# A gated two-layer MLP on one core: another order of the weight and x loads, matmuls on zeros at the start, transposes between the output blocks, and the last store in two halves

## The chip, the cores and the metric

The kernel runs on one core of one Trainium2 chip. The metric is device time in microseconds. All matmuls are done by TensorE (PE), which loads a 128x128 tile of one operand (PEld in the profile) and streams up to 512 columns of the other past it into PSUM. VectorE (DVE) and ScalarE (ACT) carry results from PSUM to SBUF, GpSimd (POOL) issues the loads, SyncE (SP) the stores.

## The reference

```python
# x: 16 x 256 x 512, w1: 512 x 4096, w2: 2048 x 512, all float32
h = x @ w1
gate, value = np.split(h, 2, axis=-1)
h = np.maximum(gate, 0) * value
return (h @ w2).astype(np.float32)
```

## The kernel before

The 16 x 256 tokens are taken as 4096 rows, in eight tiles of 512 (`TOK`). The program is written for the whole loop `for t in range(NT)`, without a hardware loop, and all matmuls are in fp16.

Both weights stay in SBUF. GpSimd's DMA converts float32 to fp16 on the way. It reads w1 in eight chunks of 512 columns (L74; chunks 0 to 3 are the gate half, 4 to 7 the value half), w2 in four chunks of 512 rows (L78), and x in tiles of 512 rows (L69). Each such load reads 1 MB and leaves 0.5 MB in SBUF. They stand in one queue, in the order of lines 87 to 104: x tile 0, w1 chunks 0 and 4, x tile 1, w1 1 and 5, x tile 2, w1 2 and 6, w2 0, x tile 3, w1 3 and 7, w2 1 to 3. GpSimd has eight semaphores for them, so that it issues the ninth load once the first has landed, and so on. x tiles 4 to 7 are asked for in the loop (L110), two tiles ahead; three buffers hold them.

A tile goes through three stages on PE:

- Transposes (L119): 16 of 128x128, four for each 128 columns of x. Four go into one PSUM tile `pt`, of which there are two, and DVE copies it into `xT` (L127).
- Stage 1 (L130 to L160): 16 blocks of 128 hidden columns. A block has four `pgate` matmuls, which ScalarE turns into `relu_sb` (L142), and four `pval` matmuls, which DVE multiplies with it into `g_sb` (L155). Blocks 0 to 3 need w1 chunks 0 and 4, blocks 4 to 7 chunks 1 and 5, and so on.
- Output stage (L162 to L177): four blocks `po` of 128 rows, each 16 matmuls of `g_sb` with w2 (L165), copied by ScalarE (L173) and stored by SP (L175). Matmuls 0 to 3 of a block need w2 chunk 0, matmuls 12 to 15 chunk 3.

Each engine runs its own instructions in the order in which a scheduler has put them, which is nearly that of the code; it lets a few matmuls of stage 1 slip in between the last transposes of a tile.

Of the kernel before, what the change touches and what calls it, by code (L numbers as in the profile page):

```python
# [11 lines left out]
BF16 = mybir.dt.bfloat16  # L12

MM_DT = FP16
STORE_ENGINE = "sync"


@with_exitstack
def kernel(
# [28 lines left out]

    const_pool = ctx.enter_context(tc.tile_pool(name="const", bufs=1))
    w_pool = ctx.enter_context(tc.tile_pool(name="weights", bufs=1))  # L50
    xf_pool = ctx.enter_context(tc.tile_pool(name="x_f16", bufs=3))
    xt_pool = ctx.enter_context(tc.tile_pool(name="xT", bufs=3))
    g_pool = ctx.enter_context(tc.tile_pool(name="g", bufs=2))
    r_pool = ctx.enter_context(tc.tile_pool(name="relu", bufs=6))
    o_pool = ctx.enter_context(tc.tile_pool(name="out_sb", bufs=6))
# [4 lines left out]

    identity = const_pool.tile([P, P], MM_DT, name="identity")
    make_identity(nc, identity)

    w1_sb = w_pool.tile([P, DB, H2], MM_DT, name="w1_sb")
    w2_sb = w_pool.tile([P, JB, C], MM_DT, name="w2_sb")

    def load_x_tile(t):
        x_f16 = xf_pool.tile([P, TB, D], MM_DT, name="x_f16")
        nc.gpsimd.dma_start(out=x_f16, in_=x_r[t])  # L69
        return x_f16  # L70

    def load_w1_chunk(ci, cols_per_chunk):
        cols = slice(ci * cols_per_chunk, (ci + 1) * cols_per_chunk)
        nc.gpsimd.dma_start(out=w1_sb[:, :, cols], in_=w1_r[:, :, cols])  # L74

    def load_w2_chunk(ci, jbs_per_chunk):
        jbs = slice(ci * jbs_per_chunk, (ci + 1) * jbs_per_chunk)
        nc.gpsimd.dma_start(out=w2_sb[:, jbs, :], in_=w2_r[:, jbs, :])  # L78

    W1_CHUNKS = 8  # L80
    w1_cols = H2 // W1_CHUNKS
    W2_CHUNKS = 4
    w2_jbs = JB // W2_CHUNKS

    x_tiles = {}

    x_tiles[0] = load_x_tile(0)
    load_w1_chunk(0, w1_cols)
    load_w1_chunk(4, w1_cols)
    if NT > 1:  # L90
        x_tiles[1] = load_x_tile(1)
    load_w1_chunk(1, w1_cols)
    load_w1_chunk(5, w1_cols)
    if NT > 2:
        x_tiles[2] = load_x_tile(2)
    load_w1_chunk(2, w1_cols)
    load_w1_chunk(6, w1_cols)
    load_w2_chunk(0, w2_jbs)
    if NT > 3:
        x_tiles[3] = load_x_tile(3)  # L100
    load_w1_chunk(3, w1_cols)
    load_w1_chunk(7, w1_cols)
    for ci in range(1, W2_CHUNKS):
        load_w2_chunk(ci, w2_jbs)

    for t in range(NT):
        if t not in x_tiles:
            x_tiles[t] = load_x_tile(t)
        for tp in (t + 1, t + 2):
            if tp < NT and tp not in x_tiles:  # L110
                x_tiles[tp] = load_x_tile(tp)

        x_f16 = x_tiles.pop(t)

        xT = xt_pool.tile([P, DB, TOK], MM_DT, name="xT")
        for db in range(DB):
            pt = pt_pool.tile([P, TB, P], MM_DT, name="pt")
            for tb in range(TB):
                nc.tensor.matmul(  # L119
                    pt[:, tb, :],  # L120
                    x_f16[:, tb, db * P:(db + 1) * P],
                    identity,
                    is_transpose=True,
                    start=(tb == 0),
                    stop=(tb == TB - 1),
                )
            nc.vector.tensor_copy(out=xT[:, db, :], in_=pt[:, :, :])  # L127

        g_sb = g_pool.tile([P, JB, TOK], MM_DT, name="g_sb")
        for jg in range(JB):  # L130
            pgate = ph_pool.tile([P, TOK], FP32, name="pgate")
            pval = ph_pool.tile([P, TOK], FP32, name="pval")
            for db in range(DB):
                nc.tensor.matmul(  # L134
                    pgate,
                    w1_sb[:, db, jg * P:(jg + 1) * P],
                    xT[:, db, :],
                    start=(db == 0),
                    stop=(db == DB - 1),
                )  # L140
            relu_sb = r_pool.tile([P, TOK], MM_DT, name="relu_sb")
            nc.scalar.activation(  # L142
                out=relu_sb,
                in_=pgate,
                func=mybir.ActivationFunctionType.Relu,
            )
            for db in range(DB):
                nc.tensor.matmul(  # L148
                    pval,
                    w1_sb[:, db, (JB + jg) * P:(JB + jg + 1) * P],  # L150
                    xT[:, db, :],
                    start=(db == 0),
                    stop=(db == DB - 1),
                )
            nc.vector.tensor_tensor(  # L155
                out=g_sb[:, jg, :],
                in0=relu_sb,
                in1=pval,
                op=mybir.AluOpType.mult,
            )  # L160

        for tb in range(TB):  # L162
            po = po_pool.tile([P, C], FP32, name="po")
            for jb in range(JB):
                nc.tensor.matmul(  # L165
# [4 lines left out]
                    stop=(jb == JB - 1),  # L170
                )
            out_sb = o_pool.tile([P, C], FP32, name="out_sb")
            nc.scalar.copy(out=out_sb, in_=po)  # L173
            if STORE_ENGINE == "sync":
                nc.sync.dma_start(out=out_r[t, :, tb, :], in_=out_sb)  # L175
            else:
                nc.gpsimd.dma_start(out=out_r[t, :, tb, :], in_=out_sb)  # L177


# [28 lines left out]
```

## Time and profile before

| | |
|---|---|
| device time, median of 4 runs | 365.66 us (364.35 to 366.6) |
| the profiled execution | 364.35 us |
| its span, first to last instruction | 362.4 us |
| PE matmul / weight load busy | 343.7 us (95%) / 158.1 us (44%) |
| DVE / ACT / POOL busy | 100.9 us / 96.4 us / 15.6 us |
| 128x512 matmuls, transposes | 1536, 128 |
| moved by DMA | 19.12 MB |

The profile shows one execution. A matmul's recorded time is longer than the time after which the next one starts, since they overlap in the array; so what a run of matmuls costs is read from the starts, and not from the mean of one. The timeline gives those starts, merged where instructions of one group follow each other. The chain that ended last gives, step by step from the end, what each piece of work waited for.

### The profile page before, as it was taken

What the parts mean: (1) busy time and instruction counts of PE and PEld (TensorE: products, weight loads), DVE (VectorE), ACT (ScalarE), POOL (GpSimd) and SP (SyncE); (2) the same over time, 40 slices, a digit from 0 to 9 for tenths busy, and PEclk for the clock granted to TensorE, in tenths of its full rate; (3) what the DMA queues carried; (4) which work ended last, traced back from release to release, by engine and by line L of the source; (5) the groups of instructions that cost most, each with busy time, mean ns of one, the idle gap of its engine ahead of it and who ended that gap; (6) DMA issues with size and microseconds to landing.
All of it is one profiled execution on the core that took longest, in us unless ns stands there. A gap on an engine that the chain in (4) does not pass through costs nothing.

```text
span 362.4 us, 4054 instructions
## 1 busy us (share of the span) xinstructions
PE 343.7 (95%) x1664; PEld 158.1 (44%) x1664; DVE 100.9 (28%) x160; ACT 96.4 (27%) x161; POOL 15.6 (4%) x26
## 2 busy tenths in 40 slices
PE   2996799999999999999999999999999999999996
PEld 1332344444444444444444444444444444444442
DVE  1333202333034420433113440243304332034400
ACT  1222212332123321333113331233212331133311
POOL 8320000000000000000000000000000000000000
PEclk9999999999999999999999999999999999999999
DMA  7999912300150002400023001100020000100002
GB/s 122 204 195 207 195 57 72 51 1 3 58 115 2 0 0 89 87 0 2 29 87 60 0 2 58 58 4 0 0 82 36 0 2 29 58 31 0 0 31 87
DMA packets 15185, 19.12 MB, mean 53 GB/s; under 512 B 832, under 2 KB 11072, under 8 KB 15168
## 3 DMA queue, kind: packets, MB, share of 16 engines
q0 software_dynamic: 10560, 10.49, 17.8%
q1 hardware_dynamic: 4608, 8.39, 6.1%
q8 instruction: 13, 0.21, 0.2%
q14 instruction: 4, 0.03, 0.0%
HBM read 20.97 MB, written 8.39 MB: 81 GB/s over the span
## 4 chain that ended last, share of the span: by engine, by line
PE 87%; DMA 9%; POOL 1%; DVE 1%; issue 0%; ACT 0%; POOLq 0%
PE po L165 30%; PE pval L148 28%; PE pgate L134 27%; DMA w_sb<-in_w_dram 9%; PE pt L119 2%; DVE xT L127 1%; POOL x_f L69 0%; POOL w_sb L74 0%; ACT out_sb L173 0%; POOL identity masks.py:199 0%; POOL identity masks.py:197 0%; POOLq masks.py:199 0%; POOLq L192 0%
## 5 line engine op out<-in xcount | busy, mean ns | idle before, releaser
L134 PE MATMUL pgate<-xT,w_sb 128*128 128x512 f16 x512 | 135.5, 384 | 2.2 <-DMA w_sb<-in_w_dram 2.2
L148 PE MATMUL pval<-xT,w_sb 128*128 128x512 f16 x512 | 132.5, 380 | 3.7 <-DMA w_sb<-in_w_dram 3.7
L155 DVE TENSOR_TENSOR g_sb<-relu_sb,pval 128x512 f16<-128x512 f16 x128 | 88.0, 687 | 142.9 <-PE pval L148 142.9
L142 ACT ACTIVATE relu_sb<-pgate 128x512 f16<-128x512 f32 x128 | 76.4, 597 | 163.8 <-PE pgate L134 163.8
L165 PE MATMUL po<-w_sb,g_sb 128*128 128x512 f16 x512 | 111.8, 380 | 0.0
L148 PEld LDWEIGHTS <-w_sb 128*128 128x128 f16 x512 | 49.8, 98 | 65.5 <-DMA w_sb<-in_w_dram 5.2
L134 PEld LDWEIGHTS <-w_sb 128*128 128x128 f16 x512 | 49.8, 98 | 61.5 <-DMA w_sb<-in_w_dram 3.3
L165 PEld LDWEIGHTS <-g_sb 128*128 128x128 f16 x512 | 50.0, 98 | 60.5
L173 ACT COPY out_sb<-po 128x512 f32<-128x512 f32 x32 | 18.7, 585 | 98.6 <-PE po L165 98.6
L127 DVE COPY xT<-pt 128x512 f16<-128x512 f16 x32 | 12.9, 422 | 102.1 <-PE pt L119 101.0
L119 PE MATMUL pt<-identity,x_f 128*128 128x128 f16 x128 | 11.7, 230 | 9.3 <-DMA x_f<-in_x_dram 7.1
L119 PEld LDWEIGHTS <-x_f 128*128 128x128 f16 x128 | 9.3, 103 | 12.8 <-DMA x_f<-in_x_dram 7.1
L69 POOL DMA_DIRECT2D x_f<-in_x_dram x8 | 6.1, 766 | 162.6 <-PE pt L119 160.3
L74 POOL DMA_DIRECT2D w_sb<-in_w_dram x8 | 6.0, 767 | 3.4 <-DMA w_sb<-in_w_dram 1.9
L78 POOL DMA_DIRECT2D w_sb<-in_w_dram x4 | 3.0, 741 | 7.9 <-DMA w_sb<-in_w_dram 5.2
L142 ACT ACT_TABLE_LOAD x1 | 1.3, 1283 | 0.7 <-PEq L192 0.7
masks.py:199 POOL TENSOR_SCALAR_AFFINE_SELECT identity<-identity 128x128 f16<-128x128 f16 x1 | 0.3, 305 | 0.1
masks.py:197 POOL MEMSET identity<- 128x128 f16 x1 | 0.2, 204 | 0.3 <-POOLq L192 0.3
L192 POOL MEMSET const-float32-0.0<- 128x1 f32 x1 | 0.1, 98 | 0.2 <-issue 0.2
L192 POOL MEMSET const-bfloat16-1.0<- 128x1 bf16 x1 | 0.1, 101 | 0.0
L192 POOL MEMSET const-uint8-127<- 128x1 uint8 x1 | 0.1, 101 | 0.0
L192 POOL MEMSET const-float32-1.0<- 128x1 f32 x1 | 0.1, 98 | 0.0
## 6 DMA issues: line engine op xcount, KB each, us to landing
out_dram<-out_sb SPq DMA_DIRECT2D x32, 256.0 KB, 2.0
w_sb<-in_w_dram POOLq DMA_DIRECT2D x12, 512.0 KB, 20.5
x_f<-in_x_dram POOLq DMA_DIRECT2D x8, 512.0 KB, 5.8
```

The costliest lines, as they stand in the source:

```text
L69: nc.gpsimd.dma_start(out=x_f16, in_=x_r[t])
L74: nc.gpsimd.dma_start(out=w1_sb[:, :, cols], in_=w1_r[:, :, cols])
L78: nc.gpsimd.dma_start(out=w2_sb[:, jbs, :], in_=w2_r[:, jbs, :])
L119: nc.tensor.matmul(pt[:, tb, :], x_f16[:, tb, db * P:(db + 1) * P], identity, is_transpose=True, start=(tb == 0), stop=(tb == TB - 1),)
L127: nc.vector.tensor_copy(out=xT[:, db, :], in_=pt[:, :, :])
L134: nc.tensor.matmul(pgate, w1_sb[:, db, jg * P:(jg + 1) * P], xT[:, db, :], start=(db == 0), stop=(db == DB - 1),)
L142: nc.scalar.activation(out=relu_sb, in_=pgate, func=mybir.ActivationFunctionType.Relu,)
L148: nc.tensor.matmul(pval, w1_sb[:, db, (JB + jg) * P:(JB + jg + 1) * P], xT[:, db, :], start=(db == 0), stop=(db == DB - 1),)
L155: nc.vector.tensor_tensor(out=g_sb[:, jg, :], in0=relu_sb, in1=pval, op=mybir.AluOpType.mult,)
L165: nc.tensor.matmul(po, g_sb[:, jb, tb * P:(tb + 1) * P], w2_sb[:, jb, :], start=(jb == 0), stop=(jb == JB - 1),)
L173: nc.scalar.copy(out=out_sb, in_=po)
L192: nc = _bacc.Bacc("TRN2", target_bir_lowering=False, num_devices=1)
```

## The change

- The order of the loads. Now it is x tile 0, all w1 chunks in the order 0, 4, 1, 5, 2, 6, 3, 7, w2 chunk 0, x tile 1, w2 chunks 1 to 3, x tile 2. x tiles 3 to 7 are asked for in the loop.
- DVE clears a tile `zeros` of 128x512, and PE multiplies it with itself 18 times ahead of the first transposes and 4 times behind them in the code, into a `pgate` buffer that nobody reads (`keep_warm`).
- The transposes of tile t+1 move from the start of tile t+1 into the output stage of tile t: four ahead of each `po` block (`transpose_group`). `xT` has two buffers instead of three.
- The last `po` block of the program is copied and stored in two halves of 256 columns. The copies of the output are left to the scheduler's choice of engine; it gives all of them to ScalarE, as before.
- `load_w1_chunk_staged` and its pool are defined, but nothing calls the function.

```diff
@@ -12,7 +12,6 @@
 BF16 = mybir.dt.bfloat16
 
 MM_DT = FP16
-STORE_ENGINE = "sync"
 
 
 @with_exitstack
@@ -48,8 +47,9 @@
 
     const_pool = ctx.enter_context(tc.tile_pool(name="const", bufs=1))
     w_pool = ctx.enter_context(tc.tile_pool(name="weights", bufs=1))
+    wst_pool = ctx.enter_context(tc.tile_pool(name="w_stage", bufs=2))
     xf_pool = ctx.enter_context(tc.tile_pool(name="x_f16", bufs=3))
-    xt_pool = ctx.enter_context(tc.tile_pool(name="xT", bufs=3))
+    xt_pool = ctx.enter_context(tc.tile_pool(name="xT", bufs=2))
     g_pool = ctx.enter_context(tc.tile_pool(name="g", bufs=2))
     r_pool = ctx.enter_context(tc.tile_pool(name="relu", bufs=6))
     o_pool = ctx.enter_context(tc.tile_pool(name="out_sb", bufs=6))
@@ -60,6 +60,14 @@
 
     identity = const_pool.tile([P, P], MM_DT, name="identity")
     make_identity(nc, identity)
+    zeros = const_pool.tile([P, 512], MM_DT, name="zeros")
+    nc.vector.memset(zeros, 0.0)
+
+    def keep_warm(n):
+        dummy = ph_pool.tile([P, TOK], FP32, name="pgate")
+        for _ in range(n):
+            nc.tensor.matmul(dummy, zeros[:, :P], zeros, start=True, stop=True)
+
 
     w1_sb = w_pool.tile([P, DB, H2], MM_DT, name="w1_sb")
     w2_sb = w_pool.tile([P, JB, C], MM_DT, name="w2_sb")
@@ -69,62 +77,61 @@
         nc.gpsimd.dma_start(out=x_f16, in_=x_r[t])
         return x_f16
 
-    def load_w1_chunk(ci, cols_per_chunk):
-        cols = slice(ci * cols_per_chunk, (ci + 1) * cols_per_chunk)
+    w1_cols = 512
+    W1_CHUNKS = H2 // w1_cols
+
+    def load_w1_chunk_swdge(ci):
+        cols = slice(ci * w1_cols, (ci + 1) * w1_cols)
         nc.gpsimd.dma_start(out=w1_sb[:, :, cols], in_=w1_r[:, :, cols])
 
-    def load_w2_chunk(ci, jbs_per_chunk):
-        jbs = slice(ci * jbs_per_chunk, (ci + 1) * jbs_per_chunk)
+    def load_w1_chunk_staged(ci):
+        cols = slice(ci * w1_cols, (ci + 1) * w1_cols)
+        w_stage = wst_pool.tile([P, DB, w1_cols], FP32, name="w_stage")
+        nc.sync.dma_start(out=w_stage, in_=w1_r[:, :, cols])
+        nc.any.tensor_copy(out=w1_sb[:, :, cols], in_=w_stage)
+
+    w2_jbs = 4
+    W2_CHUNKS = JB // w2_jbs
+
+    def load_w2_chunk_swdge(ci):
+        jbs = slice(ci * w2_jbs, (ci + 1) * w2_jbs)
         nc.gpsimd.dma_start(out=w2_sb[:, jbs, :], in_=w2_r[:, jbs, :])
 
-    W1_CHUNKS = 8
-    w1_cols = H2 // W1_CHUNKS
-    W2_CHUNKS = 4
-    w2_jbs = JB // W2_CHUNKS
-
+    def transpose_group(x_f16, xT, db):
+        pt = pt_pool.tile([P, TB, P], MM_DT, name="pt")
+        for tb in range(TB):
+            nc.tensor.matmul(
+                pt[:, tb, :],
+                x_f16[:, tb, db * P:(db + 1) * P],
+                identity,
+                is_transpose=True,
+                start=(tb == 0),
+                stop=(tb == TB - 1),
+            )
+        nc.vector.tensor_copy(out=xT[:, db, :], in_=pt[:, :, :])
+
+    keep_warm(18)
     x_tiles = {}
-
     x_tiles[0] = load_x_tile(0)
-    load_w1_chunk(0, w1_cols)
-    load_w1_chunk(4, w1_cols)
-    if NT > 1:
-        x_tiles[1] = load_x_tile(1)
-    load_w1_chunk(1, w1_cols)
-    load_w1_chunk(5, w1_cols)
+    for ci in (0, 4, 1, 5, 2, 6, 3, 7):
+        load_w1_chunk_swdge(ci)
+    load_w2_chunk_swdge(0)
+    x_tiles[1] = load_x_tile(1)
+    for ci in range(1, W2_CHUNKS):
+        load_w2_chunk_swdge(ci)
     if NT > 2:
         x_tiles[2] = load_x_tile(2)
-    load_w1_chunk(2, w1_cols)
-    load_w1_chunk(6, w1_cols)
-    load_w2_chunk(0, w2_jbs)
-    if NT > 3:
-        x_tiles[3] = load_x_tile(3)
-    load_w1_chunk(3, w1_cols)
-    load_w1_chunk(7, w1_cols)
-    for ci in range(1, W2_CHUNKS):
-        load_w2_chunk(ci, w2_jbs)
+
+    xT_cur = xt_pool.tile([P, DB, TOK], MM_DT, name="xT")
+    for db in range(DB):
+        transpose_group(x_tiles[0], xT_cur, db)
+    keep_warm(4)
+    x_tiles.pop(0)
 
     for t in range(NT):
-        if t not in x_tiles:
-            x_tiles[t] = load_x_tile(t)
         for tp in (t + 1, t + 2):
             if tp < NT and tp not in x_tiles:
                 x_tiles[tp] = load_x_tile(tp)
-
-        x_f16 = x_tiles.pop(t)
-
-        xT = xt_pool.tile([P, DB, TOK], MM_DT, name="xT")
-        for db in range(DB):
-            pt = pt_pool.tile([P, TB, P], MM_DT, name="pt")
-            for tb in range(TB):
-                nc.tensor.matmul(
-                    pt[:, tb, :],
-                    x_f16[:, tb, db * P:(db + 1) * P],
-                    identity,
-                    is_transpose=True,
-                    start=(tb == 0),
-                    stop=(tb == TB - 1),
-                )
-            nc.vector.tensor_copy(out=xT[:, db, :], in_=pt[:, :, :])
 
         g_sb = g_pool.tile([P, JB, TOK], MM_DT, name="g_sb")
         for jg in range(JB):
@@ -134,7 +141,7 @@
                 nc.tensor.matmul(
                     pgate,
                     w1_sb[:, db, jg * P:(jg + 1) * P],
-                    xT[:, db, :],
+                    xT_cur[:, db, :],
                     start=(db == 0),
                     stop=(db == DB - 1),
                 )
@@ -148,7 +155,7 @@
                 nc.tensor.matmul(
                     pval,
                     w1_sb[:, db, (JB + jg) * P:(JB + jg + 1) * P],
-                    xT[:, db, :],
+                    xT_cur[:, db, :],
                     start=(db == 0),
                     stop=(db == DB - 1),
                 )
@@ -159,7 +166,17 @@
                 op=mybir.AluOpType.mult,
             )
 
+        if t + 1 < NT:
+            xT_next = xt_pool.tile([P, DB, TOK], MM_DT, name="xT")
+            x_next = x_tiles[t + 1]
+        else:
+            xT_next = None
+
+        last_tile = t == NT - 1
         for tb in range(TB):
+            if xT_next is not None:
+                transpose_group(x_next, xT_next, tb)
+
             po = po_pool.tile([P, C], FP32, name="po")
             for jb in range(JB):
                 nc.tensor.matmul(
@@ -170,11 +187,19 @@
                     stop=(jb == JB - 1),
                 )
             out_sb = o_pool.tile([P, C], FP32, name="out_sb")
-            nc.scalar.copy(out=out_sb, in_=po)
-            if STORE_ENGINE == "sync":
+            if last_tile and tb == TB - 1:
+                half = C // 2
+                nc.any.tensor_copy(out=out_sb[:, :half], in_=po[:, :half])
+                nc.sync.dma_start(out=out_r[t, :, tb, :half], in_=out_sb[:, :half])
+                nc.any.tensor_copy(out=out_sb[:, half:], in_=po[:, half:])
+                nc.sync.dma_start(out=out_r[t, :, tb, half:], in_=out_sb[:, half:])
+            else:
+                nc.any.tensor_copy(out=out_sb, in_=po)
                 nc.sync.dma_start(out=out_r[t, :, tb, :], in_=out_sb)
-            else:
-                nc.gpsimd.dma_start(out=out_r[t, :, tb, :], in_=out_sb)
+
+        if xT_next is not None:
+            xT_cur = xT_next
+            x_tiles.pop(t + 1)
 
 
 # ---- launch: one core; inputs and outputs as the reference has them ----
```

GpSimd at the start of the program, before (`x_f` is an x tile; L74 is a chunk of w1, L78 one of w2):

```order
L69 DMA x_f_92<-in_x_dram 128x4x512
...
L74 DMA w_sb<-in_w_dram 128x4x512 x2
L69 DMA x_f_96<-in_x_dram 128x4x512
L74 DMA w_sb<-in_w_dram 128x4x512 x2
L69 DMA x_f_100<-in_x_dram 128x4x512
L74 DMA w_sb<-in_w_dram 128x4x512 x2
L78 DMA w_sb<-in_w_dram 128x4x512
L69 DMA x_f_105<-in_x_dram 128x4x512
L74 DMA w_sb<-in_w_dram 128x4x512 x2
L78 DMA w_sb<-in_w_dram 128x4x512 x3
```

And now (L77 is an x tile, L85 a chunk of w1, L98 one of w2):

```order
L77 DMA x_f_116<-in_x_dram 128x4x512
...
L85 DMA w_sb<-in_w_dram 128x4x512 x8
L98 DMA w_sb<-in_w_dram 128x4x512
L77 DMA x_f_127<-in_x_dram 128x4x512
L98 DMA w_sb<-in_w_dram 128x4x512 x3
L77 DMA x_f_132<-in_x_dram 128x4x512
L77 DMA x_f_478<-in_x_dram 128x4x512
```

The last two chunks of w1 were loads 12 and 13 of the queue and are 8 and 9; the last chunk of w2 was load 16 and is 14.

PE at the start of the program, with what it waits for (DMASW is a load, by the number of its semaphore; Pool and DVE are those engines); before, the transposes of x tile 0 and the first gate matmuls:

```order
L119 LDWEIGHTS x_f_92 [waits DMASW0_49]
L119 MATMUL pt<-identity,x_f_92 128x128 [waits Pool_49]
...
L119 MATMUL pt<-identity,x_f_92 128x128 [waits DVE_49]
...
L134 LDWEIGHTS w_sb [waits DMASW1_49]
L134 MATMUL pgate<-xT,w_sb 128x512
```

And now, where the matmuls on `zeros` stand first (22 of them, two rows each):

```order
L69 LDWEIGHTS zeros [waits DVE_49]
L69 MATMUL pgate<-zeros 128x512
...
L103 LDWEIGHTS x_f_116 [waits DMASW0_49]
L103 MATMUL pt<-identity,x_f_116 128x128 [waits Pool_49]
...
L141 LDWEIGHTS w_sb [waits DMASW1_49]
L141 MATMUL pgate<-xT,w_sb 128x512
```

All 22 matmuls on `zeros` come ahead of the first transpose, the four that are written behind the transposes too.

PE from the end of stage 1 of tile 0 to the first gate matmuls of tile 1, before, the first row of each piece (DMASW7 is the last chunk of w2; `x_f_96` is x tile 1):

```order
L148 MATMUL pval<-xT,w_sb 128x512
...
L165 MATMUL po<-w_sb,g_sb 128x512 [waits DMASW1_49]
...
L165 MATMUL po<-w_sb,g_sb 128x512 [waits DMASW7_49]
...
L165 MATMUL po<-w_sb,g_sb 128x512 [waits Activation_49]
...
L119 MATMUL pt<-identity,x_f_96 128x128 [waits PE_49]
...
L119 MATMUL pt<-identity,x_f_96 128x128 [waits DVE_49]
...
L134 MATMUL pgate<-xT,w_sb 128x512
...
L119 MATMUL pt<-identity,x_f_96 128x128 [waits DVE_49]
```

And now (DMASW5 is the last chunk of w2, DMASW2 is x tile 1, `x_f_127`):

```order
L155 MATMUL pval<-xT,w_sb 128x512
L103 LDWEIGHTS x_f_127 [waits DMASW2_49]
L103 MATMUL pt<-identity,x_f_127 128x128 [waits PE_49]
...
L182 MATMUL po<-w_sb,g_sb 128x512 [waits DMASW1_49]
...
L182 MATMUL po<-w_sb,g_sb 128x512 [waits DMASW5_49]
...
L103 MATMUL pt<-identity,x_f_127 128x128 [waits PE_49]
...
L182 MATMUL po<-w_sb,g_sb 128x512
...
L103 MATMUL pt<-identity,x_f_127 128x128 [waits DVE_49]
...
L182 MATMUL po<-w_sb,g_sb 128x512 [waits Activation_49]
...
L141 MATMUL pgate<-xT,w_sb 128x512
```

The transposes of the next tile, which came in a row behind the fourth `po` block with waits on DVE among them, now come in groups of four ahead of each block.

## Rows read from the trace of the kernel before

**Rows 1.** The page: span, PE's share, DMA's busy tenths in 40 slices of the span.

```profile
span 362.4 us, 4054 instructions
...
PE 343.7 (95%) x1664; PEld 158.1 (44%) x1664; DVE 100.9 (28%) x160; ACT 96.4 (27%) x161; POOL 15.6 (4%) x26
...
DMA  7999912300150002400023001100020000100002
```

**Rows 2.** The page: the chain that ended last, share of the span by engine.

```profile
PE 87%; DMA 9%; POOL 1%; DVE 1%; issue 0%; ACT 0%; POOLq 0%
```

**Rows 3.** The chain in order of time, whole span: start us, us, what.

```profile
4.68 12.60 DMA w_sb<-in_w_dram
17.57 21.56 DMA w_sb<-in_w_dram
...
45.40 13.81 PE po L165 x64
...
345.08 13.83 PE po L165 x64
```

**Rows 4.** Waits, whole span: us in total, times, longest.

```profile
PE pval L148 <- DMA w_sb<-in_w_dram: 3.7, 3, 1.5
...
PE pgate L134 <- DMA w_sb<-in_w_dram: 2.2, 2, 1.8
```

**Rows 5.** Timeline of the start: start us, us, engine, line, what [idle before <-releaser].

```profile
0.74 0.20 POOL masks.py:197 MEMSET identity<- 128x128 f16 x1 [0.29 <-POOLq L192]
...
2.47 1.50 POOL L74 DMA_DIRECT2D w_sb<-in_w_dram  x2
...
7.14 2.14 PE L119 MATMUL pt<-identity,x_f 128*128 128x128 f16 x16 [7.14 <-DMA x_f<-in_x_dram]
...
9.65 3.59 PE L134 MATMUL pgate<-xT,w_sb 128*128 128x512 f16 x8 [0.37 <-DMA w_sb<-in_w_dram]
...
13.04 1.95 PE L148 MATMUL pval<-xT,w_sb 128*128 128x512 f16 x8
...
20.21 0.74 POOL L78 DMA_DIRECT2D w_sb<-in_w_dram  x1 [1.90 <-DMA w_sb<-in_w_dram]
...
23.72 0.74 POOL L78 DMA_DIRECT2D w_sb<-in_w_dram  x1 [2.77 <-DMA x_f<-in_x_dram]
...
45.23 2.11 PE L165 MATMUL po<-w_sb,g_sb 128*128 128x512 f16 x9
```

**Rows 6.** DMA issues begun near 3.2 and at 20.21: KB each, us to landing.

```profile
w_sb<-in_w_dram POOLq DMA_DIRECT2D x1, 512.0 KB, 8.9
...
w_sb<-in_w_dram POOLq DMA_DIRECT2D x1, 512.0 KB, 21.5
```

**Rows 7.** The chain from 59 to 63 us, between tiles 0 and 1.

```profile
59.21 0.24 PE pt L119 x4
...
59.47 0.43 DVE xT L127
...
59.95 0.38 PE pt L119 x4
60.33 0.22 PE pgate L134
60.55 0.22 PE pt L119 x4
...
62.31 0.86 PE pgate L134 x4
```

**Rows 8.** The page, costliest groups: count | busy us, mean ns of one | idle.

```profile
L173 ACT COPY out_sb<-po 128x512 f32<-128x512 f32 x32 | 18.7, 585 | 98.6 <-PE po L165 98.6
...
L119 PE MATMUL pt<-identity,x_f 128*128 128x128 f16 x128 | 11.7, 230 | 9.3 <-DMA x_f<-in_x_dram 7.1
```

**Rows 9.** The page, DMA issues: the stores, KB each, us to landing.

```profile
out_dram<-out_sb SPq DMA_DIRECT2D x32, 256.0 KB, 2.0
```

## The prediction

> **What bounds the kernel now.** I read the page's shares first, then the chain that ended last, then the waits of TensorE (PE), and last the timeline at the three places that the change touches. TensorE is busy for 95% of the span, and the DMA engines are busy only at its start [rows 1]. The chain is 87% PE and 9% DMA [rows 2]. So two things can give time: the PE's idle time while the weights come in, and PE work between the tiles that is not a needed 128x512 matmul.
>
> From tile to tile the output matmuls (`po`) start at 45.40 in tile 0 and at 345.08 in tile 7 [rows 3]: seven periods of 42.81 us. A `po` stage takes 13.81 us for 64 matmuls, 0.2158 each; four gate matmuls take 0.86 [rows 3, 7], the same pace. A tile has 128 + 64 = 192 such matmuls, 41.44 us. **1.37 us a tile** is the boundary: sixteen transposes and their waits.
>
> At the start PE waits for weights: 3.7 us in three waits ahead of `pval`, 2.2 us in two ahead of `pgate` [rows 4]. The first eight 128x512 matmuls, from 9.65 to 13.04, run at 0.424 us each, which is 512 columns at 1.2 GHz; from 13.04 on they run at the 2.4 GHz pace [rows 5]. PE's first work was at 7.14, so the clock rose 5.9 us after it. From 13.04 the rest of stage 1 needs 8 x 0.2158 + 28 x 0.863 = 25.90 us and would end at 38.94; the first `po` starts at 45.23 [rows 5]. So stage 1 of tile 0 loses **6.29 us** to late weights (the recorded waits plus a pipeline refill after each).
>
> **Load order.** Before, the 13th of 16 equal transfers (the last w1 chunk, landing at 17.57 + 21.56 = 39.13 [rows 3]) opens the last quarter of stage 1; three of the twelve ahead of it are x tiles 1 to 3, and one is a w2 chunk. Now that chunk is the 9th. The stream is one queue of 1 MB reads, so I give a transfer the landing time of its slot. Slot 3 lands at 3.2 + 8.9 = 12.1 (its issue is the second of the two that begin at 2.47), slot 5 at 4.68 + 12.60 = 17.28, slot 14 at 20.21 + 21.5 = 41.71 [rows 3, 5, 6]: 2.69 us a slot on average.
>
> Now PE's path through tile 0. The 22 zero matmuls (the 4 that are written after the transposes stand ahead of them too in PE's program) start when VectorE (DVE) has cleared `zeros`. The trace has no such clear on DVE; the nearest rows are the GpSimd clear of `identity`, 0.20 us from 0.74 [rows 5], and a DVE copy of 128x512, 0.43 us [rows 7], so they start between 0.94 and 1.2; I take 1.1. All at the slow pace they end at 1.1 + 22 x 0.424 = 10.4, all at the fast one at 5.9. With the rise 5.9 us after the first of them, 14 are slow and 8 fast, and they end near 8.8; I take that, since the 5.9 us is this kernel's own. x tile 0 has been there since 7.14 [rows 5], so its transposes begin 1.6 us later than before, but at the fast pace: as at a boundary, 1.34 us against the 2.14 us of the start [rows 5, 7]. The gate matmuls of the first two hidden blocks run from 10.1 to 11.9 and the value matmuls then wait for slot 3, to 12.2. So **the zero matmuls buy little**: the next weight chunk hides nearly all of it (12.2 instead of 13.04).
>
> From 12.2 stage 1 needs 25.90 us if no weight is late. Slot 5 (17.28) is wanted by the value matmuls of the fifth block at 18.2; later chunks have more room, since four blocks take 6.9 us and two slots 5.4. So it ends at 38.1. The output stage begins with four transposes (0.22), and its thirteenth matmul, at 38.1 + 0.22 + 12 x 0.2158 = 40.9, wants the last w2 chunk, slot 14, at 41.7: a **new wait of 0.8 us**, and the stage is pinned to the stream there. It ends, with 52 matmuls and three more groups of transposes, at 41.71 + 11.22 + 0.66 = 53.59. Without transposes and boundary that stands for a `po` start at 53.59 - 13.81 - 0.88 = 38.90 instead of 45.23: **6.3 us gained**. Before, the tail of w2 stayed hidden behind the late w1; that cover is gone, and the 0.8 us is its price. x tile 1 is slot 11, three before slot 14 and so near 33.6, ahead of its transposes at 38.1. Later x tiles are asked for more than one tile (over 40 us) ahead, as before.
>
> **Transposes.** Before, 16 of them run in a row between two tiles, and with two PSUM banks the third group waits for DVE's copy of the first (59.45 to 59.95) and the fourth is partly filled by a gate matmul [rows 7]. Now each group of four stands before one `po` block, 3.45 us after the group before; a copy of 0.43 us is done long before its bank is wanted, and the next tile's `xT` is complete 3 us early. What a group costs there is the four matmuls themselves: 0.22 us between two gate matmuls, 0.24 after `po` [rows 7]. No row shows a group followed by `po`; the bounds are zero (all four hidden) and 0.92, four times the recorded 230 ns of a transpose [rows 8]. I take 0.22, since the row at 60.55 also has weights loaded and 512-column matmuls on both sides. So 4 x 0.22 = 0.88 instead of 1.37 at seven boundaries: **3.4 us gained**. The copies fall into DVE's idle time beside `po`.
>
> **The last store** is now two halves. ScalarE copies 128x512 in 585 ns [rows 8]; a 128x256 copy is not in the trace, and lies between half of that and all of it. Two take 0.585 to 1.17 us; I take 0.74, as a copy has some cost that does not halve. SP is free, and its 256 KB stores land 2.0 us after issue [rows 9]. So the bounds are 1.0 gained (if half the bytes land in half the time) and 0.6 lost; with the landing left at 2.0 it is **0.15 us lost**.
>
> On this the Trainium skill, "DMA: Bandwidth & Descriptors", section "Anatomy of one DMA", says that most of a small transfer's 2 us is the receipt from the target memory and not the bytes, so that a half store would land no sooner. By that rule the split can't gain anything; the 2.0 us of the trace agrees in size, and no run here has a half store.
>
> **Sum.** 6.3 + 3.4 - 0.15 = 9.6 us. The profiled execution took 364.35 us, 1.95 more than its span of 362.4, so it would take 354.8. It was the fastest of the four runs shown; their median is 1.3 us higher, and I forecast the median: 365.66 - 9.6 = **356.0 us**.
>
> **Rivals.**
>
> *The zero matmuls don't raise the clock.* Then all 22 are slow and end at 10.4; transposes (2.14) and eight gates (3.4) stay slow, the value matmuls start at 16.0, stage 1 ends at 41.9, and nothing waits for w2. Tile 0 ends at 41.9 + 13.81 + 0.88 = 56.6, 3.0 us later: 359.0. For it: no row shows a matmul on zeros. Against: before, 16 transposes and 8 matmuls raised the clock. Chance 0.10.
>
> *The stream is slower than its slots.* GpSimd, which issues the ninth and later transfers as earlier ones land, was let go at 17.57, 20.21 and 23.72 [rows 3, 5]: one step took 2.6 us, the next 3.5. At 3.1 us a slot after slot 3, slot 14 lands at 46.2, 4.5 us later: 360.5. At 2.6 it lands at 40.7, nothing waits, and it is 355.2. Chance of a loss over 2 us: 0.12.
>
> *Slower: the transposes no longer overlap their neighbours.* If every transpose between `po` blocks is paid at its recorded 230 ns, a group costs 0.92 and not 0.22 and the 28 groups lose 19.6 us: 375.6. It decides from 0.56 us a group (9.6 / 28 more), and is slower by over 0.5% from 0.63. For it: the transposes now cut the densest stretch of the kernel 28 times. Against: the 0.22 and 0.24 us of rows 7. Chance 0.03.
>
> The Trainium skill, "TensorE: Matmul & The Clock Gate", Part 4, puts a transpose at about 275 ns in a kernel's context; an estimate by that figure is 1.1 us a group, 24.6 us lost over the 28. The trace speaks against taking it as occupancy: four starts pass in 0.22 us.
>
> *It doesn't do what it says.* The new order stands in the programs of PE and GpSimd, so that only a balance of losses (a late stream and dear transposes) could leave the time where it is: within 0.5%, chance 0.03.
>
> **How the numbers follow.** The forecast has 0.72, with 353.8 to 358.0 as its own range: 0.8 for the wait on w2, 1.0 gained or 0.6 lost at the last store, some 0.5 for the transposes, and the 1.3 us by which runs differ, which will not all fall on one side. The rest goes to 359.0, 360.5, no change and slower as above. A range of 353.8 to 360.0 takes in the cold start and most of the late stream. About 0.5% is what a measurement of this kernel can tell from no change: faster than 363.8 has 0.94, the same 0.03, slower 0.03.
>
> **What would show it.** Right: PE starts near 1.1 and the fast pace holds from the first gate matmul; only slot 3 and the last w2 chunk (about 0.8 us) are waited for by PE in tile 0; tile 0's `po` ends near 53.6; a period of 42.3 us with no wait of PE on DVE; the last copies some 0.15 us longer. Wrong: waits on w1 in stage 1 (the stream), eight gate matmuls at 0.42 us after 10 us (the clock), or a period over 42.8 us (the transposes).

## The result and the profile after

| | before | after |
|---|---|---|
| median | 365.25 us (16 runs, 363.65 to 366.98) | 354.93 us (10 runs, 354.66 to 355.8) |
| ratio after / before, 95% interval | | 0.9723 [0.9699, 0.9746] |
| span of the profiled execution | 362.4 us | 353.3 us |
| PE matmul busy | 343.7 us (95%) | 346.8 us (98%) |
| first `po` matmul of tile 0 (its start; the chain has 0.17 more) | 45.23 | 39.30 |
| last `po` matmul done, by the chain | 358.91 | 349.40 |
| from there to the end of the span | 3.49 us | 3.90 us |

The changed kernel is 10.3 us faster by the medians, and 9.1 us by the two spans. 356.0 us (353.8 to 360.0) was forecast; it came to 354.93.

The page after, its span, PE's row, the DMA slices and the chain by engine, beside [rows 1, 2]:

```profile
span 353.3 us, 4109 instructions
...
PE 346.8 (98%) x1686; PEld 160.0 (45%) x1686; DVE 101.0 (29%) x161; ACT 96.6 (27%) x162; POOL 15.6 (4%) x26
...
DMA  7999934000420006000150001100020000100011
...
PE 95%; DMA 3%; POOL 1%; ACT 0%; issue 0%; POOLq 0%
```

DMA's part of the chain has shrunk from 9% to 3%: it is what PE waits for at the start, once. The chain of tile 0 in order of time (start us, us, what), beside [rows 3, 7]:

```profile
3.22 9.90 DMA w_sb<-in_w_dram
...
13.17 1.90 PE pval L155 x8
...
39.24 0.22 PE pt L103 x4
39.47 3.45 PE po L182 x16
42.92 0.22 PE pt L103 x4
...
53.95 0.86 PE pgate L141 x4
...
81.80 3.45 PE po L182 x16
```

One load (`w_sb`, issued at 3.22) and then PE without a gap. From the `po` at 39.47 to the one at 81.80, tile 0 to tile 1, is 42.33 us; it was 42.81. Each group of four transposes takes 0.22 us between two `po` blocks, and there are no waits among them.

The start of the timeline (PE's matmuls, and three of the weight loads on zeros), beside [rows 5]:

```profile
1.19 7.47 PE L69 MATMUL pgate<-zeros 128*128 128x512 f16 x22 [1.19 <-DVE zeros L64]
...
1.60 0.15 PEld L69 LDWEIGHTS <-zeros 128*128 128x128 f16 x1 [0.28 <-issue]
2.02 0.15 PEld L69 LDWEIGHTS <-zeros 128*128 128x128 f16 x1 [0.28 <-issue]
...
6.29 1.88 PEld L69 LDWEIGHTS <-zeros 128*128 128x128 f16 x9 [0.28 <-issue]
...
8.50 0.61 PE L103 MATMUL pt<-identity,x_f 128*128 128x128 f16 x8
...
10.19 1.90 PE L141 MATMUL pgate<-xT,w_sb 128*128 128x512 f16 x8
...
13.17 1.90 PE L155 MATMUL pval<-xT,w_sb 128*128 128x512 f16 x8 [1.08 <-DMA w_sb<-in_w_dram]
```

PE now starts at 1.19. The weight loads on zeros come every 0.43 us (1.60, 2.02, ...) until 6.29, and then nine in 1.88 us: that is 1.2 GHz and then 2.4 GHz, some 5.1 us after the first matmul. The transposes and the first gate matmuls (8 in 1.90) run at the fast pace. Then PE waits 1.08 us for the third load, until 13.17. The waits of PE for loads over the whole span, beside [rows 4]:

```profile
PE pval L155 <- DMA w_sb<-in_w_dram: 1.1, 1, 1.1
```

Five waits were 5.9 us together; one of 1.1 us is left. The wait on the last w2 chunk, which was forecast, isn't there.

### The profile page after: what moved, and what is told of

Same layout as the page of the kernel before. It is cut to its first block, busy times and chain, and to the rows that moved or that the text cites. A ratio compares the mean times of both kernels' runs of the same rounds, so it can differ in the third digit from the quotient of the medians.

```text
span 353.3 us, 4109 instructions
## 1 busy us (share of the span) xinstructions
PE 346.8 (98%) x1686; PEld 160.0 (45%) x1686; DVE 101.0 (29%) x161; ACT 96.6 (27%) x162; POOL 15.6 (4%) x26
## 4 chain that ended last, share of the span: by engine, by line
PE 95%; DMA 3%; POOL 1%; ACT 0%; issue 0%; POOLq 0%
PE pval L155 31%; PE po L182 31%; PE pgate L141 31%; DMA w_sb<-in_w_dram 3%; PE pt L103 2%; POOL x_f L77 0%; POOL w_sb L85 0%; ACT out_sb L192 0%; ACT out_sb L194 0%; POOL identity masks.py:199 0%; POOL identity masks.py:197 0%; POOLq masks.py:199 0%; POOLq L217 0%
## 5 line engine op out<-in xcount | busy, mean ns | idle before, releaser
L141 PE MATMUL pgate<-xT,w_sb 128*128 128x512 f16 x512 | 131.3, 380 | 0.1
L182 PE MATMUL po<-w_sb,g_sb 128*128 128x512 f16 x512 | 115.3, 380 | 0.0
L182 PEld LDWEIGHTS <-g_sb 128*128 128x128 f16 x512 | 48.9, 98 | 53.8
L77 POOL DMA_DIRECT2D x_f<-in_x_dram x8 | 6.1, 758 | 154.9 <-PE pt L103 148.4
L69 PE MATMUL pgate<-zeros 128*128 128x512 f16 x22 | 7.5, 520 | 1.2 <-DVE zeros L64 1.2
L85 POOL DMA_DIRECT2D w_sb<-in_w_dram x8 | 6.0, 775 | 0.0
L69 PEld LDWEIGHTS <-zeros 128*128 128x128 f16 x22 | 2.7, 128 | 5.4 <-issue 3.3
L98 POOL DMA_DIRECT2D w_sb<-in_w_dram x4 | 3.0, 741 | 7.4 <-DMA w_sb<-in_w_dram 7.4
L192 ACT COPY out_sb<-po 128x256 f32<-128x256 f32 x1 | 0.4, 372 | 2.9 <-PE po L182 2.9
L194 ACT COPY out_sb<-po 128x256 f32<-128x256 f32 x1 | 0.4, 373 | 0.0
```

What stands on the lines that cost most here:

```text
L69: nc.tensor.matmul(dummy, zeros[:, :P], zeros, start=True, stop=True)
L141: nc.tensor.matmul(pgate, w1_sb[:, db, jg * P:(jg + 1) * P], xT_cur[:, db, :], start=(db == 0), stop=(db == DB - 1),)
L182: nc.tensor.matmul(po, g_sb[:, jb, tb * P:(tb + 1) * P], w2_sb[:, jb, :], start=(jb == 0), stop=(jb == JB - 1),)
```

## The experiments

All times are medians; the kernel before ran beside each of them on the same chip. Its runs spread by 3 to 4.3 us every time, so the lowest runs are compared beside the medians; what the spread is made of comes further down.

**The load order alone** (in the kernel before):

```diff
-    load_w1_chunk(4, w1_cols); x_tiles[1] = load_x_tile(1); load_w1_chunk(1, w1_cols) ...
+    for ci in (0, 4, 1, 5, 2, 6, 3, 7):
+        load_w1_chunk(ci, w1_cols)
+    load_w2_chunk(0, w2_jbs); x_tiles[1] = load_x_tile(1)
+    for ci in range(1, W2_CHUNKS): load_w2_chunk(ci, w2_jbs)
+    x_tiles[2] = load_x_tile(2)
```

> The kernel before with the new order of the loads alone. If late weights cost tile 0 its 6.3 us, stage 1 now waits only at its first blocks, the first output matmul starts at 39 to 39.2 instead of 45.23, the last w2 chunk is waited for by at most 0.3 us, the tile period stays 42.81, and the time falls by 6.0 to 6.3 us (ratio 0.983). If the zero matmuls and the fast clock at the start are what lets PE use the earlier weights, the gain is under 5 us (ratio above 0.986).

357.99 us against 366.46, ratio 0.9791 [0.9742, 0.984]; lowest run 357.86 against 363.93, 6.1 us. The profiled run was the slowest of its four (359.48; the others, which have no profile, 357.86 to 358.1), and its timeline shows a reason:

```profile
7.25 2.14 PE L109 MATMUL pt<-identity,x_f 128*128 128x128 f16 x16 [7.25 <-DMA x_f<-in_x_dram]
...
10.18 3.59 PE L124 MATMUL pgate<-xT,w_sb 128*128 128x512 f16 x8 [0.79 <-DMA w_sb<-in_w_dram]
...
13.56 2.78 PE L138 MATMUL pval<-xT,w_sb 128*128 128x512 f16 x8
```

The eight value matmuls took 2.78 us and not 1.90: about four of them still ran at the slow pace, to some 8 us after PE's first transpose at 7.25. In this run `po` begins at 40.35, 4.9 us sooner than before and not the 6.0 to 6.2 that were expected. No wait on w1 follows, and the period stays 42.81. So the load order alone, without zero matmuls, is worth 6.1 us in the lowest runs; the 8.5 us between the medians holds more than that, which is taken up below.

**The transposes alone** (the changed kernel with the old load order, no zero matmuls, one last store):

```diff
-    keep_warm(18)
-    for ci in (0, 4, 1, 5, 2, 6, 3, 7): ...
+    (the loads as in lines 87 to 104 of the kernel before)
-    keep_warm(4)
```

> The kernel before with only the transposes moved between the output blocks (old load order, no zero matmuls, one last store). If the boundary was worth 1.37 and a group of four costs 0.22, the period is 42.32 instead of 42.81 and the time falls by 3.4 us (ratio 0.9907); tile 0 still loses its 6.3 us to w1. If a transpose between output blocks is paid at its recorded 230 ns, the period is 45.1 and the time rises by 16 us.

361.73 us against 366.46, ratio 0.9884 [0.983, 0.9938]; lowest run 360.39 against 363.93, 3.5 us. The chain, at the output stages of tile 0 and 1:

```profile
45.21 3.45 PE po L184 x16
48.66 0.22 PE pt L101 x4
48.88 3.45 PE po L184 x16
...
87.32 0.22 PE pt L101 x4
87.54 2.59 PE po L184 x12
```

The period is 87.54 - 45.21 = 42.33. The boundary has gone from 1.37 to 0.89, and the rival that pays each transpose at its recorded 230 ns (45.1) is out. Tile 0 still starts its `po` at 45. The two parts add up: 6.1 + 3.5 is near the 6.3 + 3.4 of the sum, and the kernel with both, the zeros and one last store (below) has its lowest run 9.8 us under that of the kernel before.

**Without the zero matmuls** (the changed kernel):

```diff
-    zeros = const_pool.tile([P, 512], MM_DT, name="zeros")
-    nc.vector.memset(zeros, 0.0)
-    keep_warm(18)
-    keep_warm(4)
```

> The changed kernel without the zero matmuls and without the clear of the zeros tile. In the changed kernel the value matmuls began at 13.17, since the third load landed at 13.1 and not at 12.1. Theory A (the third load lands at 13.1 whatever PE does, because a weight chunk and not an x tile follows it): the eight slow gate matmuls end at 13.05, nothing is lost, the time stays within 0.3 us. Theory B (the clear on DVE or the matmuls on zeros delayed the loads by 1 us): the third load lands near 12.1 again, the value matmuls start at 13.05, the time falls by 0.1 us or stays. Rival (the fast clock is worth what it saved on PE, 8 x 0.21 + 0.8 = 2.5 us): the time rises by 2 us or more.

355.65 us (354.67 to 356.34); the profiled run, 354.68 with a span of 352.7, began its value matmuls at 12.41. There the third load landed at 12.4; with zeros and the same loads it landed at 12.5 in the next experiment and at 13.1 in the changed kernel's profile. So the 1 us belongs neither to the clear nor to the zero matmuls (theory B), nor is it fixed by the order (theory A): it differs from run to run. The rival (2 us worse) is out by the lowest run, which equals that of the changed kernel (354.67 and 354.66). The median is 0.7 us higher, though, and the spread is 1.7 us; both come back below.

**One last store:**

```diff
-            if last_tile and tb == TB - 1:
-                ... two copies and two stores of 256 columns
-            else:
-                nc.any.tensor_copy(out=out_sb, in_=po)
+            nc.scalar.copy(out=out_sb, in_=po)
```

> The changed kernel with the last block copied and stored in one piece. The changed kernel took 3.9 us from the last matmul to the end, the kernel before 3.5. If the two halves cost that, the end is 3.5 again and the time falls by 0.4 us; by the prediction it falls by 0.15 us. If the halves help (the store of the first half runs beside the second copy), the time rises.

354.23 us (354.12 to 354.33), the fastest of these four kernels. The changed kernel itself (354.93) did not run beside it, so the ends of the two profiles are compared. The timeline of the changed kernel's last copies on ScalarE and stores on SP:

```profile
349.43 0.37 ACT L192 COPY out_sb<-po 128x256 f32<-128x256 f32 x1 [2.87 <-PE po L182]
349.82 0.33 SPq L193 DMA_DIRECT2D out_dram<-out_sb  x1
349.83 0.37 ACT L194 COPY out_sb<-po 128x256 f32<-128x256 f32 x1
350.25 0.38 SPq L195 DMA_DIRECT2D out_dram<-out_sb  x1
```

and its last DMA issue (KB, us to landing):

```profile
out_dram<-out_sb SPq DMA_DIRECT2D x1, 128.0 KB, 1.8
```

The same two views with one store:

```profile
348.83 0.59 ACT L190 COPY out_sb<-po 128x512 f32<-128x512 f32 x1 [2.87 <-PE po L182]
...
349.44 0.33 SPq L191 DMA_DIRECT2D out_dram<-out_sb  x1
```

```profile
out_dram<-out_sb SPq DMA_DIRECT2D x1, 256.0 KB, 2.0
```

A half copy takes 0.37 us, so the second store is issued 0.85 us after the last matmul (349.40 to 350.25) and not 0.63 (348.81 to 349.44). It lands in 1.8 us instead of 2.0. But from its landing at 352.05 to the end of the span it is 1.25 us, against 0.86 (351.44 to 352.3). The end takes 3.90 us with halves and 3.49 with one store. What the span does in the last 0.4 us no row shows.

**Is it the zeros, with the store out of the way?** The one-store kernel once more, and the same without the clear and the 22 matmuls (the edit of the third experiment):

> The changed kernel with one last store, once more, as the kernel that the other three are compared with on the same chip: 354.2 us as before, within 0.5 us between its runs.

> The same without the clear of the zeros tile and without the 22 matmuls on it. Theory C (the clock rises at a moment that differs from run to run; the zeros take that out of the start): the fastest run is within 0.3 us of the kernel with zeros, the median is 0.5 to 1.2 us above it, and the runs spread by over 1 us. Theory A (the third load hides the slow gates in every run): median within 0.2 us, the same spread.

With zeros 354.52 us (354.45 to 355.32, 4 runs), without 354.42 (354.2 to 356.3, 5 runs); against the kernel before 0.9697 [0.9668, 0.9727] and 0.9704 [0.9673, 0.9736]. No difference in the median; of the runs without, two of five are over 355.5, of those with none of four. In the two profiles the value matmuls began at 12.78 (waiting for the load) and 12.70 (slow gates, then no wait). **In such runs the zero matmuls are worth nothing**, since the load hides what they save. That is theory A, and the median agrees with it. Theory C is right about the lowest runs and the spread: the wide kernels are those without zeros. Of the third experiment and this one, 6 of 11 runs without zeros lie more than 0.8 us (a bound set afterwards) above the lowest run of their kernel; with zeros and the same loads it is 2 of 21. In the third experiment that moved the median: 355.65 against 354.23 with one store is 1.4 us, and the store explains 0.4. The profile of the load order alone shows how such a run comes about, with value matmuls at the slow pace. So the zeros seem to take out late starts; no such run of these kernels has a profile, and whether that is worth 0 or 1 us of the median these runs leave open.

**A start that needs less weight.** If the third load is what PE waits for, halves of the first chunks should let it start sooner, and only then the zeros could matter:

```diff
-    for ci in (0, 4, 1, 5, 2, 6, 3, 7):
-        load_w1_chunk_swdge(ci)
-    load_w2_chunk_swdge(0); x_tiles[1] = load_x_tile(1)
+    for c0 in (0, 256, 512, 768):
+        load_w1_half(c0); load_w1_half(H + c0)      # 256 columns each
+    for ci in (2, 6, 3, 7): load_w1_chunk_swdge(ci)
+    for ci in range(W2_CHUNKS): load_w2_chunk_swdge(ci)
+    x_tiles[1] = load_x_tile(1)
-    keep_warm(18); keep_warm(4)
+    keep_warm(16)
```

In tile 0 the transposes of tile 1 stand eight at a time ahead of the third and the fourth `po` block.

> One last store, 16 matmuls on zeros; the first two column pairs of w1 are read in halves of 256 columns, so that the first value matmuls need 2 MB of loads and not 3; x tile 1 comes behind w2, and its transposes stand ahead of the third and fourth output block. If PE's start is bound by the third load, the value matmuls start near 10.4 instead of 12.5, no later wait takes it back, and the time falls by 1.5 to 2.5 us against f1. Rival (512-byte pieces are read slower, or the stream catches PE again at the fifth block or at w2): the gain is under 0.7 us or a loss.

> The same without the clear and the matmuls on zeros. Now no load hides the slow clock: the transposes run from 7.2, eight gate and value matmuls at 0.42 us, and PE loses 1.5 to 3 us against f3 unless the clock happens to rise early. If the zeros are worth nothing here either, the two are within 0.3 us.

With zeros 353.31 us (352.96 to 353.94), ratio to before 0.9661 [0.9631, 0.9691]: 1.2 us faster than the one-store kernel beside it, and the fastest kernel of this study. Less than forecast, and the timeline has the reason:

```profile
8.75 1.04 PE L145 MATMUL pgate<-xT,w_sb 128*128 128x512 f16 x4 [0.16 <-DMA w_sb<-in_w_dram]
...
10.09 1.04 PE L159 MATMUL pval<-xT,w_sb 128*128 128x512 f16 x4 [0.30 <-DMA w_sb<-in_w_dram]
...
24.73 1.04 PE L159 MATMUL pval<-xT,w_sb 128*128 128x512 f16 x4 [0.66 <-DMA w_sb<-in_w_dram]
```

The first value matmuls start at 10.09 instead of 12.78. That is 2.7 us sooner, but four gate matmuls stand ahead of them and not eight, so PE's work is only 1.8 us further on (four take 0.86). And PE waits 0.66 us at 24.73 for w1 chunk 6, which was issued at 10.32 and landed 14.4 us later; the load ahead of it had landed at 20.6 (8.99 + 11.6), so this one step of the stream took 4.1 us. The other waits are 0.5 us together. `po` begins at 37.70; in the one-store kernel it began at 38.91 with 0.22 of transposes ahead of it, so 1.0 us is left. Without zeros it was 353.89 (353.4 to 354.68), where a loss of 1.5 to 3 us was expected unless the clock rose early. In its profile it did: the first four gate matmuls took 1.87 us, the value matmuls ran at the fast pace from 10.93, 3.7 us after PE's first transpose, and PE came to chunk 6 without a wait, so that `po` began at 37.72. A gain of 0.6 us by the zeros is what the medians say, and the intervals (0.9631 to 0.9691 and 0.9652 to 0.9711) overlap.

**The kernel before, profiled twice more, and with the zeros.** Its medians had been 0.9 to 2.1 us above its profiled run of 364.35.

> The kernel before, profiled once more. Its runs lie between 363.7 and 368.3, those of the changed kernel within 1.2 us. Theory S (the late weights expose the stream: a slow step of the loads goes straight into the time): the last w1 chunk lands later or earlier than 39.2 and the first output matmul moves with it, 6.0 us behind; periods stay 42.81. Theory K (the clock): matmuls at 0.42 us at another place than the first eight.

> The kernel before, profiled a third time; the two theories expect what they expect of the second.

Both took 365.6 us, with a span of 363.7. Windows of the first (us, busy of each engine, PEclk is the granted clock, then DMA share and GB/s), and then of its last stretch in the profile of before that the prediction used:

```profile
33.80:36.20 2.40, 1.04 (x5) 0.29 (x3) 0.80 (x2) 0.60 (x1) 0.00 (x0) 1.00 1.24 206
36.20:38.80 2.60, 1.04 (x4) 0.31 (x4) 0.00 (x0) 0.60 (x1) 0.00 (x0) 1.00 1.24 206
38.80:42.20 3.40, 3.40 (x9) 1.19 (x10) 0.69 (x1) 0.00 (x0) 0.00 (x0) 0.50 1.24 206
```

```profile
38.80:42.20 3.40, 3.02 (x14) 1.38 (x15) 0.84 (x2) 0.60 (x1) 0.00 (x0) 1.00 1.24 206
```

and the timeline of the first of the two:

```profile
36.22 1.04 PE L134 MATMUL pgate<-xT,w_sb 128*128 128x512 f16 x4 [1.38 <-DMA w_sb<-in_w_dram]
...
38.80 1.89 PE L148 MATMUL pval<-xT,w_sb 128*128 128x512 f16 x4 [1.55 <-DMA w_sb<-in_w_dram]
...
40.48 1.89 PE L134 MATMUL pgate<-xT,w_sb 128*128 128x512 f16 x4
...
42.19 1.04 PE L148 MATMUL pval<-xT,w_sb 128*128 128x512 f16 x4
```

The same two places in the profile that the prediction used:

```profile
36.67 1.04 PE L134 MATMUL pgate<-xT,w_sb 128*128 128x512 f16 x4 [1.84 <-DMA w_sb<-in_w_dram]
39.18 1.04 PE L148 MATMUL pval<-xT,w_sb 128*128 128x512 f16 x4 [1.47 <-DMA w_sb<-in_w_dram]
```

Behind the two waits on the last w1 chunks the granted clock is 0.50 for 3.4 us, and eight matmuls take 3.39 us instead of 1.73. The other new profile shows the same fall, at 38.76, behind 1.36 and 1.54 us. The profile that the prediction used waits at the same two places, 1.84 and 1.47 us, and its clock stays up; and so does the clock of the kernel with zeros, next, behind 1.36 and 1.54 us. So late weights have a **second price**: 1.7 us in some executions, where the clock falls behind the waits. What decides between the two no row shows.

How often it is paid can be read from the mean granted clock, which is on record for every run of these experiments beside its time. 3.4 us at half lower the mean over a span of 363.7 us by 0.005. The two new profiles have a mean of 0.994 and 0.995, the first one 0.998. The 54 runs of the kernel before in these experiments fall into three groups:

| mean granted clock | runs | time | median |
|---|---|---|---|
| 0.998 to 1.000 | 20 | 363.4 to 364.7 us | 364.2 us |
| 0.994 or 0.995 | 16 | 364.5 to 366.4 us | 365.7 us |
| 0.991 | 18 | 366.1 to 368.3 us | 366.7 us |

The middle group fits one such fall. A mean of 0.991 is some 6 us at half, by an estimate (0.009 x 366.7 us, doubled), so more than one; no run of that group has a profile. Between the first and the last group lie 2.5 us, inside a group 1.3 to 2.2 us. So about half of the spread of the kernel before goes with the clock. In the changed kernel all 11 runs have 0.998 or more. Like against like, the load order alone is worth 6.0 us (357.99, all four at 0.999 or more, against 363.98) and the transposes 3.5 us (360.4 against 363.98) or, at 0.991, 3.9 us (363.0 against 366.9).

The kernel before with the clear and 22 matmuls on zeros at the start:

> The kernel before with the clear and 22 matmuls on zeros alone. In the old load order the last w1 chunk sets the end of stage 1, whatever PE's clock did at the start: the time stays within 0.5 us of the kernel before, and its runs spread by 3 us as those of before do. If the spread of before comes from the clock at the start, the spread shrinks below 1 us and the median falls by 1 us or more.

364.36 us (363.38 to 366.01) against 365.09, ratio 0.9984 [0.9956, 1.0012], no difference; the spread is 2.6 us. What PE's clock does in the first 13 us is of no weight while a later load sets the end of stage 1. Only 3 of these 12 runs have a mean clock of 0.995 or less, beside 10 of 17 of the kernel before; why fewer is open.

**Work in the waits.** If the fall behind the waits is the spread of the kernel before, PE work in the waits should take it away:

```diff
+            if t == 0 and jg in (4, 8, 12):     # and ahead of pgate for 8 and 12
+                fill(6, g_sb, jg - 1)           # 6 matmuls of g_sb with itself, into an unread po
             for db in range(DB):
                 nc.tensor.matmul(pval, ...
```

> The kernel before, with six extra matmuls that nobody reads (1.3 us) ahead of each of the five places in stage 1 of tile 0 where PE waits for a w1 chunk, so that PE is at work in most of the wait. Two further profiles of the kernel before showed the clock at half for 3.4 us behind the wait on the last w1 chunk, the first output matmul 1.3 us later, a span of 363.7. Theory K (the waits let the clock fall in some runs, and that is the spread of the kernel before): the median comes to 363.9 within 0.3 us, no run is above 365, the eight matmuls behind the last chunk take 1.73 us. Theory S (the loads themselves differ from run to run): the spread stays at 3 us and the median within 0.4 us of the kernel before.

364.95 us (364.04 to 366.16) against 365.31 (363.67 to 367.38), ratio 0.9994 [0.997, 1.0017]. Neither theory as a whole: the spread went from 3.7 to 2.1 us, the highest run came down by 1.2 and the lowest rose by 0.4. In its profile the clock stays up and PE is busy throughout from 33.8 to 42.2, but the five fills (6.5 us) are as long as all the waits were, so that PE hardly waits and its own start (eight gate matmuls at the slow pace from 10.18, value matmuls from 13.57) goes into the time: `po` begins at 47.1. So the edit was too large to show a gain. But its clocks answer the question: all 12 runs have a mean of 0.998 or more, where 9 of the 17 of the kernel before beside them have 0.995 or less. Work in the waits does take the fall away, as theory K has it, and the 2.1 us of spread that are left are not falls of this kind.

## Why the prediction was right, point by point

**Load order, 6.3 us.** Right in size: 6.1 us by the load order alone. Inside it two terms were off and balanced. The third load landed at 13.1 and not at 12.1, so that the value matmuls began 1.0 us late; in five other profiles with the new order it landed between 12.4 and 12.8. And the last w2 chunk, put at 41.71, landed at 21.04 + 20.1 = 41.1, while the later start wanted it at 39.30 + 12 x 0.2158 = 41.9: the forecast wait of 0.8 us became none. Tile 0's last `po` block started at 50.33 by the timeline, and with 16 x 0.2158 us ended at 53.8; 53.59 was forecast. The prediction had called the stage pinned to the stream; it was pinned at its other end, by the third load. That the two errors nearly cancelled is luck. Without zeros, where the third load landed at 12.4, PE did stand still for 0.15 us ahead of the matmul of `po` that wants the last w2 chunk, and went on at 41.29, as that chunk landed (20.25 + 21.0; the view names no releaser); the last block started at 49.72, 0.6 us sooner. So where the start is on time the forecast wait seems to come, but smaller than 0.8.

**The zero matmuls buy little.** Right for the profiled run: the transposes behind them began at 8.50 (8.7 forecast), the clock had risen, so the first rival is out, and the third load hides the gain. The sum gave them no part in the spread; the runs without them are the wider ones, by up to 1 us of a median.

**Transposes, 3.4 us.** Right: a group costs 0.22, the period is 42.33 (42.32 forecast), 3.5 us by itself. The 275 ns of the Trainium skill ("TensorE: Matmul & The Clock Gate", Part 4) is nearer to the recorded duration of a transpose (219 ns after) than to the time that PE gives to it here, 55 ns; the measurement decides.

**The last store, 0.15 us lost.** Right in sign, too small: 0.41. The copies cost 0.22 (0.15 forecast), the landing gave back 0.2, and 0.4 came behind the landing, which was not in the sum. The section of the Trainium skill that the prediction drew on ("DMA: Bandwidth & Descriptors", "Anatomy of one DMA") puts most of the 2 us on the receipt, but it describes GpSimd's path, and these stores are SP's; and it has a term for the bytes besides, by which an estimate for half of this store is 0.3 us less. So "no sooner" did not follow from it. Measured, half the bytes saved 0.2 of 2.0 us.

**The sum.** From span to span 9.6 us were forecast and 9.1 came (0.2 less in tile 0, 0.26 less at the end). **The step that was off was the last one**, from the profiled execution to the median. I gave the changed kernel the same 1.3 us above its profiled run that the kernel before had; in fact its median, 354.93, is 0.5 below its profiled run of 355.46. That 1.3 us is the kernel before's own, and it goes with the clock. By the 54 runs above (those of the kernel before in the table of the result have none on record), the runs with a mean of 0.998 or more have a median of 364.2, near the profiled run of 364.35, and the others lie 1.5 and 2.5 us higher. Against 364.2 the changed kernel gains 9.3 us, close to the sum. The other 1.0 us of the 10.3 between the medians goes with falls of the clock, which none of the 11 runs of the changed kernel shows; in its profile PE has no wait on a load behind 13.2 us. The prediction read one execution, in which the clock had stayed up, and took the distance to the median for one that would stay.

**The late-stream rival** didn't come about as a whole, but its slow steps did: 3.0 us twice at the start of the changed kernel's stream, 4.1 us once with the halves.

## What to carry to other kernels

Order loads by when the bound engine wants them, and then ask which load is late next: here it was the third one at the start, and halves of the first chunks gave 1.2 us more. A warm-up on zeros gains nothing in a run where a load ends later than it does, so see what the first real matmul waits for before adding one; what it can still do is take out the runs in which the clock rises late. When the runs of a kernel spread more than its profile explains, put the mean granted clock of each run beside its time: a gain that is read from one execution leaves out what its waits cost in the others.

## What the runs showed of the hardware

The granted clock of TensorE fell to half for 3.4 us behind waits of 1.38 and 1.55 us with four matmuls between them, in two of three profiles of one kernel. It stayed up behind waits of 1.84 and 1.47 us in the third, and behind 1.36 and 1.54 us in the kernel with zeros at the start. Going by the mean clock (0.995 or less), 34 of 54 runs of that kernel had at least one such fall, and with matmuls put into the waits none of 12 had.

From PE's first work to the fast pace it took 5.1 us in the changed kernel, 5.9 in the first profile of the kernel before, about 8 us in the profile of the load order alone, and 3.7 with halves and no zeros. At the start the granted clock stands at 1.00 in the rows even where matmuls run at 0.424 us each, so there only the starts of the matmuls tell the clock. The windows of the kernel with halves and no zeros, around the four gate matmuls that take 1.87 us (PEclk is the number behind the last bracket):

```profile
9.25:10.90 1.65, 1.65 (x5) 0.53 (x5) 0.55 (x2) 0.00 (x0) 0.84 (x2) 1.00 1.37 177
10.90:13.00 2.10, 2.10 (x11) 1.01 (x10) 0.69 (x1) 0.71 (x2) 1.39 (x2) 1.00 1.45 196
```

Loads of 1 MB in one queue land 2.3 to 2.8 us apart for the most part, but single steps took 3.0, 3.5 and 4.1 us, at other places in each run, with 189 to 208 GB/s moved in these steps.
